# The output product of the mixers: attention's blocks first, other PSUM banks, weight splits on VectorE

## The chip, the cores and the metric

The kernel runs on one core of a Trainium2 chip. The core has a matrix engine (TensorE, PE in the rows, its weight loads PEld) and three engines for elementwise work: VectorE (DVE), ScalarE (ACT) and GpSimd (POOL). SyncE (SP) issues the DMA transfers. Each engine runs its own queue in order and waits for the others by semaphores. The metric is the device time of one execution in microseconds; lower is better.

## The reference, cut to what matters

Two decoder layers on 512 tokens of width 1024, in float32. A layer is four sub-steps, each between two RMS norms and added to x:

```python
x += 1/2 * post(swiglu_a(pre(x)))
h  = pre(x) @ W_in            # columns for attention | mLSTM | RWKV-7
x += post(concat(attn, mlstm, rwkv) @ W_out)
x += 1/2 * post(swiglu_b(pre(x)))
x += post(sigmoid(pre(x) @ W_g) * (p[l] @ W_p))
```

The concatenated output of the mixers has 1024 columns: 512 of attention, 256 of the mLSTM, 256 of RWKV-7. With the 1024 x 1024 matrix `W_out` it makes the output product, which is the place of the change.

## The kernel before, in words

Each float32 operand of a product is split in a high part, rounded to the reduced format fp32r, and a low rest. `split` (L138) has ScalarE round the high part (L139) and another engine, VectorE unless `eng` says GpSimd, subtract it (L140). `mm3` (L165) is then three matmuls: high by high (L167), high by low (L168), low by high (L169). Tokens lie in four tiles of 128.

The mixers of a layer run woven into each other (`weave`, L649): attention, RWKV's scan over chunks and the mLSTM each issue pieces in turn, each with PSUM banks of its own. There are eight banks, by tags: `m` has two, `r` three, and `o`, `a` and `b` one each. `lanes(main, aux)` sets the two cycles of tags from which `mm_tile` and `aux_tile` take the next bank; without arguments they are `mmoa` and `brrr` (L27). During the weave, attention uses `o`, `a` and `b`, the scan and the mLSTM `m` and `r`. The results are split into `yh` and `yl` (xh, xl in the rows), two chunks of 128 rows for each quarter of `W_out`: quarters 0 and 1 are attention's, 2 the mLSTM's, 3 RWKV's. RWKV's last steps are the norm (`rwkv_norm`, L952 to L957), transposes (`rwkv_back`, L964), a gate (L968 to L973) and the split into `yh` and `yl`; the mLSTM's last steps are L1206 to L1219 and its transposes, `pym` (L1136). Working data of all this lies in the `arena`, which is given back at the end.

`out_proj` (L262) makes the product in two halves of 512 output columns. For half 0 each of the four token tiles has an accumulator `y0`, for half 1 `y1`. In half 0 the first three blocks are loaded, split and multiplied with all four token tiles; the last block (`wot`) goes tile by tile, so that the tiles finish one after the other. In half 1 all four blocks go tile by tile; their raw weights `wor` lie in slots which overlap the arena, as do the raw weights `wr` of the next feed-forward, so both loads wait for the arena's last reader. `orders` in `mix` gives the order of the quarters in each half. `OW` (L31) has one letter for each block of half 0: with "1" the low half of its weights is made on GpSimd.

When a tile of y1 is done, `out_evac` squares and sums it on ScalarE (L196) and multiplies it by the gain on VectorE (L259); `postnorm` gets the factor r on GpSimd (`rms`, L185 and L186) and adds to x on VectorE (L254). Then `prenorm` squares and sums x (L196), gets r (L186), multiplies (L207, `xn`), and `turn` transposes (L218, `xtp`) and splits. For tiles 2 and 3, `turn` also makes sums of x (`xr`, `tx`: L239 to L242) and splits them for the feed-forward, whose products use sums of blocks in the manner of Strassen. There, for each unit of 128 columns, `gate` makes `p12`, `unit` makes the sums of weights (L355, L357, L358), splits them (`w75`, `w63`) and makes `p63`, `p75` and `p4`. `ffn_begin` loads the first units' weights (`wr`) and splits them (`w1`, the low halves on GpSimd).

The order of the instructions is not the program's: a scheduler orders them from its own timeline of the program, by when operands and buffers are ready in it. So an edit at one place can move instructions at others.

Of the kernel before, what the change touches and what calls it, by code (L numbers as in the profile page):

```python
# [27 lines left out]

CONSTS, NCONST = {}, 0
MX = 1  # L30
OW = "1111"  # L31
PL = "000021"
TORD = (0, 2, 1, 3)
FSEQ = [[(q[0], int(q[1:])) for q in f.split()] for f in ("P0 S3 S4 P1 S5 S6 P2 S7 S8 S9", "S6 S7 S8 S9 S3 S4 S5")]
# [38 lines left out]
class Trunk:  # L73
# [188 lines left out]
    def out_proj(self, nb, part, blocks, gain, scale, after, tail):  # L262

        half0 = []
        for h in range(2):
# [8 lines left out]
            for i in range(cut):  # L274
                w, a = self.wblock(blocks(h, i), "wo", eng=self.nc.gpsimd if h == 0 and OW[i] == "1" else None), part(h, i)
                for t in range(NT):
                    one(i, w, a, t)
            raws = [None] * nb
            if h and tail == nb:
                raws = [q[:, j] for q in [self.slot("q", [2, 1024], "wor") for _ in range(nb // 2)] for j in range(2)]  # L280
            rest = [(i, self.wblock(blocks(h, i), "wot", bool(h), raws[i], self.nc.gpsimd if (raws[i] is not None and OE[i] == "1" if h else OW[i] == "1") else None), part(h, i)) for i in range(cut, nb)]
            def finish(t):
                e = self.out_evac(ps[t], gain, h, scale)
                if h == 0:
                    half0.append(e)
                else:
                    self.postnorm(t, half0[t], e, scale)
                    self.late.append(after(t))
# [298 lines left out]
    def mix(self, l, after):  # L587
        nc, tc = self.nc, self.tc
        self.yh, self.yl = self.xh, self.xl
        self.close_slots()  # L590
        xd = self.dram.tile([NT, 128, D], F32, tag="xd", name="xd")
        for t in range(NT):
            nc.sync.dma_start(out=xd[t], in_=self.x[:, t])
        self.xs = self.x.rearrange("p a b -> p (a b)")
        with tc.tile_pool(name="arena", bufs=1) as pa:
            self.arena = pa.tile([128, 16384], F32, name="arena")
            cs = self.region(0, [SLOT])
            o = 0

            def load(n, ap):  # L600
                nonlocal o
                t = cs[:, o:o + n]
                nc.sync.dma_start(out=t, in_=ap)
                o += n
                return t

            self.pf = pf = load(38, self.ins["mix_cols"][l])
            self.consts = load(NCONST, self.ins["consts"])
            self.rows = load(272, self.ins["mix_rows"][l:l + 1].to_broadcast([128, 272]))
            self.gup = load(256, self.ins["rwkv_g_up"][l])  # L610
            self.om = om = cs[:, o:o + 10]
            assert o + 10 <= SLOT
            nc.vector.scalar_tensor_tensor(self.cen, self.const("bones"), -1.0 / 64, self.ident, ALU.mult, ALU.add)
            nc.vector.tensor_scalar(om[:, 0:8], pf[:, 0:8], -1.0, 1.0, op0=ALU.mult, op1=ALU.add)
            nc.vector.tensor_scalar(om[:, 8:10], pf[:, 14:16], -1.0, 1.0, op0=ALU.mult, op1=ALU.add)
            with tc.tile_pool(name="arena2", bufs=1) as pb:
                self.arena2 = pb.tile([128, 6144], F32, name="arena2")
                self.lanes("oab")
                self.attention_kv(l)
                with tc.tile_pool(name="keys", bufs=1) as pk:  # L620
                    self.bkt = pk.tile([128, 2048], F32, name="bk")
                    self.lanes("m", "r", "R")
                    self.rwkv_prep(l)
                    self.lanes("oab")
                    self.attention_q(l)
                    self.lanes("m", "r", "R")
                    self.mg = self.gains.tile([128, D], F32, tag="gain", name="mg")
                    self.rwkv_scores()
                with tc.tile_pool(name="parts", bufs=1) as pk:
                    self.parts = pk.tile([128, 2048], F32R, name="parts")  # L630
                    self.mlstm_proj(l)
                    self.weave(l)
        for t in range(NT):
            nc.sync.dma_start(out=self.x[:, t], in_=xd[t])
        self.open_slots()
        self.lanes()
        wo = self.ins["w_out"]
        post = self.gain("ln_mix_post", l)
        if not self.dbg:
            orders = ((2, 0, 1, 3), (3, 2, 0, 1))  # L640
            self.out_proj(4, lambda h, i: [[q[:, 2 * orders[h][i] + j] for q in (self.yh, self.yl)] for j in range(2)],
                          lambda h, i: wo[l, h, orders[h][i]], post, 1.0, after, 4)
        else:
            for t in range(8):
                o = self.ytile()
                nc.vector.tensor_tensor(o, self.yh[:, t].bitcast(F32), self.yl[:, t].bitcast(F32), ALU.add)
                nc.sync.dma_start(out=self.out[:, t], in_=o)
# [866 lines left out]
```

## Time and profile before

| | |
|---|---|
| median of 3 runs | 2187.12 us (2185.07 to 2189.22) |
| profiled execution | 2185.51 us |
| its span | 2183.8 us |
| granted clock of PE, mean | 0.989 |
| busy PE / DVE / ACT / POOL | 97% / 79% / 46% / 15% |

The times are the median of three runs; the trace is from one execution, whose own time is 1.6 us below the median. Its span goes from the first to the last instruction. A row of the timeline gives the start, the duration, engine, source line, operation and tiles; in square brackets stands how long the engine had been idle before it and what ended that. Rows that overlap on one engine are pipelined; the distance of their starts is what one costs.

### The profile page before, as it was taken

Reading aid. Unit: us, or ns where it says so; the run is one execution under the profiler, and the core shown is the slowest. Engines: PE = TensorE matmul, PEld = TensorE weight load, DVE = VectorE, ACT = ScalarE, POOL = GpSimd, SP = SyncE. Lnnn points to the kernel's source line nnn. Section 1 sums busy time; section 2 is a strip of 40 time slices with the busy share of each in tenths; the row PEclk is TensorE's granted clock in tenths of the full one; section 3 lists DMA queues with packets and bytes.
Section 4 is the critical chain, followed back from the end, with each engine's and each line's share of the span. In section 5 each row is a group of like instructions: output and inputs, shape, how many; then the busy total and the mean of one; then the engine's idle time right before and its main releaser. Section 6 shows DMA issues by size and latency. Waiting matters only on the chain.

```text
span 2183.8 us, 39815 instructions
## 1 busy us (share of the span) xinstructions
PE 2108.5 (97%) x16256; PEld 1959.2 (90%) x16256; DVE 1718.1 (79%) x2886; ACT 1007.5 (46%) x1653; POOL 330.5 (15%) x424
## 2 busy tenths in 40 slices
PE   6999999999988999999979999999999989999998
PEld 5999999888767999999879999998886789999996
DVE  8999977555768999977689999775557689999774
ACT  4444434446545444434554444345465454444343
POOL 4000011132235000011240000110422340000111
PEclk8999999999999999999989999999999999999999
DMA  4322214322031232224313222252210413222241
GB/s 164 117 97 99 86 68 154 122 71 57 21 141 53 103 111 97 88 68 165 115 58 117 97 98 78 79 178 97 64 54 12 155 59 117 97 97 78 78 143 71
DMA packets 67495, 208.62 MB, mean 96 GB/s; under 512 B 15728, under 2 KB 16752, under 8 KB 67312
## 3 DMA queue, kind: packets, MB, share of 16 engines
q1 hardware_dynamic: 67312, 206.07, 26.9%
q8 instruction: 128, 2.10, 0.4%
q14 instruction: 55, 0.45, 0.1%
HBM read 199.23 MB, written 6.82 MB: 94 GB/s over the span
## 4 chain that ended last, share of the span: by engine, by line
PE 81%; DVE 9%; ACT 3%; DMA 3%; issue 2%; POOL 2%; SPq 0%; DVEq 0%; POOLq 0%; ACTq 0%
PE y L463 18%; PE p L169 13%; PE p L168 13%; PE p L167 13%; PE pkrv L169 1%; PE pkrv L168 1%; PE pkrv L167 1%; PE y L167 1%; PE y L168 1%; PE y L169 1%; DVE xn L207 1%; DMA ws_r<-in_w_ffn_out 1%; DVE w L140 1%; PE pgt L168 1%; PE pgt L169 1%
## 5 line engine op out<-in xcount | busy, mean ns | idle before, releaser
L169 PE MATMUL p<-xh,w 128*128 128x256 f32 x1408 | 401.1, 286 | 7.5 <-POOL w L140 7.5
L167 PE MATMUL p<-xh,w 128*128 128x256 f32 x1408 | 401.2, 286 | 4.4 <-DVE gate L367 2.4
L168 PE MATMUL p<-xl,w 128*128 128x256 f32 x1408 | 401.1, 285 | 0.4 <-DVE xl L140 0.4
L167 PE MATMUL p<-tx,w 128*128 128x256 f32 x1056 | 295.9, 284 | 9.6 <-ACT tx L139 8.0
L168 PE MATMUL p<-tx,w 128*128 128x256 f32 x1056 | 295.3, 283 | 6.5 <-DVE tx L140 6.5
L169 PE MATMUL p<-tx,w 128*128 128x256 f32 x1056 | 294.9, 283 | 2.5 <-DVE w L140 2.5
L169 PEld LDWEIGHTS p<-xh,w 128*128 128x128 f32 x1408 | 271.9, 193 | 8.1 <-POOL w L140 8.1
L167 PEld LDWEIGHTS p<-xh,w 128*128 128x128 f32 x1408 | 271.7, 194 | 6.7 <-DVE gate L367 3.2
L168 PEld LDWEIGHTS p<-xl,w 128*128 128x128 f32 x1408 | 271.9, 193 | 1.4 <-DVE xl L140 1.3
L139 ACT ACTIVATE w<-ws 128x1024 fp32r<-128x1024 f32 x176 | 185.9, 1056 | 159.0 <-PE p L169 144.2
L140 DVE TENSOR_TENSOR w<-ws,w 128x1024 fp32r<-128x1024 f32 x176 | 221.3, 1257 | 15.8 <-ACT w L139 15.0
L167 PEld LDWEIGHTS p<-tx,w 128*128 128x128 f32 x1056 | 201.7, 192 | 12.0 <-ACT tx L139 9.2
L168 PEld LDWEIGHTS p<-tx,w 128*128 128x128 f32 x1056 | 201.9, 192 | 7.5 <-DVE tx L140 7.5
L169 PEld LDWEIGHTS p<-tx,w 128*128 128x128 f32 x1056 | 200.6, 191 | 2.8 <-DVE w L140 2.8
L139 ACT ACTIVATE w<-wr 128x512 fp32r<-128x512 f32 (+1 forms) x176 | 147.8, 844 | 113.8 <-PE p L169 66.7
L463 PE MATMUL y<-wo,hq 128*128 128x256 f32 x1536 | 193.3, 283 | 0.0
L463 PEld LDWEIGHTS y<-wo,hq 128*128 128x128 f32 x1536 | 186.4, 190 | 0.8
L499 POOL TENSOR_TENSOR tb<-tb,ln_ffn_post 128x512 f32<-128x512 f32 x16 | 24.1, 1530 | 1076.5 <-ACT junk L196 1076.5
L463 PE MATMUL y<-ws_r,h 128*128 128x256 f32 x672 | 158.4, 379 | 0.2
L140 DVE TENSOR_TENSOR w<-wr,w 128x512 fp32r<-128x512 f32 (+1 forms) x161 | 151.4, 943 | 5.6 <-ACT w L139 4.7
L463 PEld LDWEIGHTS y<-ws_r,h 128*128 128x128 f32 x672 | 121.2, 189 | 14.7 <-DMA ws_r<-in_w_ffn_out 0.8
L351 ACT ACTIVATE gate<-p 128x256 f32<-128x256 f32 x88 | 33.1, 381 | 171.6 <-PE p L169 169.4
(426 smaller groups left out, 4766.8 us busy)
## 6 DMA issues: line engine op xcount, KB each, us to landing
wr<-in_w_ffn_in SPq DMA_DIRECT2D x176, 512.0 KB, 4.1
ws_r<-in_w_ffn_out SPq DMA_DIRECT2D x56, 512.0 KB, 3.3
wo_r<-in_w_ffn_out SPq DMA_DIRECT2D x32, 512.0 KB, 3.3
pkrv_r<-in_w_rw SPq DMA_DIRECT2D x16, 512.0 KB, 3.5
wpg_r<-in_w_ple_gate SPq DMA_DIRECT2D x16, 512.0 KB, 4.0
xd<-x SPq DMA_DIRECT2D x8, 512.0 KB, 2.8
x<-xd SPq DMA_DIRECT2D x8, 512.0 KB, 3.5
pq_r<-in_w_q SPq DMA_DIRECT2D x8, 512.0 KB, 3.5
```

Of the source, the lines that this page charges most:

```text
L139: self.nc.scalar.activation(hi, src, AF.Copy)
L140: (eng or self.nc.vector).tensor_tensor(lo, src, hi.bitcast(F32), ALU.subtract)
L167: mm(out, a[0], b[0], start=first, stop=False)
L168: mm(out, a[0], b[1], start=False, stop=False)
L169: mm(out, a[1], b[0], start=False, stop=last)
L207: v_.scalar_tensor_tensor(xn[:, h], self.x[:, t, h], r, gain[:, h], ALU.mult, ALU.mult)
L351: a_.activation(a[:, (H, L)[m % 2]], pa[:, L], AF.Copy)
L463: nc.tensor.matmul(banks[n][:, u], x, y, start=n not in seen, stop=last and i == len(todo) - 1, skip_group_check=True)
L499: (g_ if not h or QL[0] == "1" else v_).tensor_tensor(tb, tb, gain[:, h * 512:h * 512 + 512], ALU.mult)
```

## The change

Three edits, in both layers. The letters of `OW` become "0000": the low halves of half 0's four weight blocks are made on VectorE. The order of half 0's quarters becomes 0, 1, 3, 2 (attention, attention, RWKV, mLSTM) from 2, 0, 1, 3. And the accumulators get other banks: y0 of tiles 0 to 3 in `o`, `a`, `b`, `m` (before `m`, `m`, `o`, `a`), y1 in `m`, `r`, `r`, `r` (before `b`, `r`, `r`, `r`); after the product the lanes are set back.

```diff
-OW = "1111"
+OW = "0000"
...
-        self.lanes()
+
+        self.lanes("oabm", "mrrr")
         wo = self.ins["w_out"]
         post = self.gain("ln_mix_post", l)
         if not self.dbg:
-            orders = ((2, 0, 1, 3), (3, 2, 0, 1))
+            orders = ((0, 1, 3, 2), (3, 2, 0, 1))
             self.out_proj(4, lambda h, i: [[q[:, 2 * orders[h][i] + j] for q in (self.yh, self.yl)] for j in range(2)],
                           lambda h, i: wo[l, h, orders[h][i]], post, 1.0, after, 4)
+            self.lanes()
```

The lines of the kernel after are one higher from L637 and two higher from L644 on. In the rows below the number behind a name tells its uses apart: `y0_6809` to `y0_6812` are half 0's sums of token tiles 0 to 3 in layer 0, `wo_6815`, `wo_6844` and `wo_6873` its first three blocks of weights.

On PE, at the end of the mixers of layer 0. Before, the product begins behind the last step of the RWKV scan (`py_6693`) and the mLSTM's transposes:

```order
L925 MATMUL py_6693<-st_6033,arena_4195 64x128
L905 MATMUL pq_6688<-st_6033,arena_4195 64x128
L1172 MATMUL pnum_6763<-vg_5176,arena_4195 128x128 x3
L1178 MATMUL pint_6768<-arena_4195 128x130 x2
L927 MATMUL py_6693<-arena2_4206 64x64 x2
L925 MATMUL py_6693<-st_6033,arena_4195 64x128
L927 MATMUL py_6693<-arena2_4206 64x64 x2
L1136 MATMUL pym_6787<-ident_78,mg_4923 128x128 x2
L167 MATMUL y0_6811<-wo_6815,xh_87 128x512
L168 MATMUL y0_6811<-wo_6815,xh_87 128x512
```

After, it begins further up, at attention's last values (`po_5990`), ahead of the state steps `pq_6627` and `py_6641` of the scan, of which two more follow:

```order
L917 MATMUL pst_6626<-st_6033,ident_78 64x128
L1370 MATMUL po_5990<-arena_4195 64x512
L167 MATMUL y0_6810<-wo_6815,xh_87 128x512
L168 MATMUL y0_6810<-wo_6815,xh_87 128x512
L169 MATMUL y0_6810<-wo_6815,xl_88 128x512
L167 MATMUL y0_6810<-wo_6815,xh_87 128x512
L168 MATMUL y0_6810<-wo_6815,xh_87 128x512
L169 MATMUL y0_6810<-wo_6815,xl_88 128x512
L167 MATMUL y0_6810<-wo_6844,xh_87 128x512
L168 MATMUL y0_6810<-wo_6844,xh_87 128x512
L169 MATMUL y0_6810<-wo_6844,xl_88 128x512
```

Thirty-six products of attention's two blocks with tiles 0 to 2 now stand ahead of the scan's last step, at four places, and 12 of the third block behind it, ahead of RWKV's transposes `pyt`. Behind the mLSTM's last transposes 174 products of both halves stood, now 144.

On DVE, between the product and the second feed-forward (`tb` is L259's product of y1 with the gain, `x_86` the sum of L254, `xn` the norm of the next sub-step for tiles 1 and 2, `xl_88` the split of transposed x). Before:

```order
L259 TENSOR_TENSOR tb_7158<-y1_6951,ln_mix_post_6807 128x512
L207 SCALAR_TENSOR_TENSOR xn_7114<-x_86,r_7111,ln_ffn2_pre_7030 128x512 x2
L140 TENSOR_TENSOR xl_88<-xtp_7117,xh_87 128x4x128
L254 SCALAR_TENSOR_TENSOR x_86<-tb_6939,r_7164,x_86 128x512
L254 SCALAR_TENSOR_TENSOR x_86<-tb_7158,r_7164,x_86 128x512
L140 TENSOR_TENSOR xl_88<-xtp_7122,xh_87 128x4x128
L259 TENSOR_TENSOR tb_7228<-y1_6952,ln_mix_post_6807 128x512
L207 SCALAR_TENSOR_TENSOR xn_7179<-x_86,r_7176,ln_ffn2_pre_7030 128x512 x2
L140 TENSOR_TENSOR xl_88<-xtp_7182,xh_87 128x4x128
L254 SCALAR_TENSOR_TENSOR x_86<-tb_6944,r_7234,x_86 128x512
```

After:

```order
L207 SCALAR_TENSOR_TENSOR xn_7114<-x_86,r_7111,ln_ffn2_pre_7030 128x512 x2
L140 TENSOR_TENSOR xl_88<-xtp_7122,xh_87 128x4x128
L259 TENSOR_TENSOR tb_7158<-y1_6951,ln_mix_post_6807 128x512
L254 SCALAR_TENSOR_TENSOR x_86<-tb_6939,r_7164,x_86 128x512
L254 SCALAR_TENSOR_TENSOR x_86<-tb_7158,r_7164,x_86 128x512
L140 TENSOR_TENSOR xl_88<-xtp_7182,xh_87 128x4x128
L207 SCALAR_TENSOR_TENSOR xn_7179<-x_86,r_7176,ln_ffn2_pre_7030 128x512 x2
L140 TENSOR_TENSOR xl_88<-xtp_7187,xh_87 128x4x128
L259 TENSOR_TENSOR tb_7228<-y1_6952,ln_mix_post_6807 128x512
L254 SCALAR_TENSOR_TENSOR x_86<-tb_6944,r_7234,x_86 128x512
L254 SCALAR_TENSOR_TENSOR x_86<-tb_7228,r_7234,x_86 128x512
```

The product L259 of tiles 2 and 3 stood ahead of the norm of the tile before it and now stands behind it.

On DVE, at the start of the second feed-forward (`tx_7208` is the split of the sums for token tiles 2 and 3, `ws_7477` and `ws_7478` are unit 1's sums of weights, `w75_7394` and `w63_7397` unit 0's splits, `w75_7482` unit 1's). Before:

```order
L140 TENSOR_TENSOR tx_7208<-tx_7211,tx_7208 128x4x128
L140 TENSOR_TENSOR xl_88<-xtp_7203,xh_87 128x4x128
L140 TENSOR_TENSOR w75_7394<-ws_7389,w75_7394 128x1024
L239 TENSOR_TENSOR xr_7127<-xr_7127,xtp_7287 128x512
L355 TENSOR_TENSOR ws_7477<-wr_7081 128x1024
L240 SCALAR_TENSOR_TENSOR tx_7297<-xtp_7292,xr_7127 128x512
L241 TENSOR_TENSOR tx_7298<-xtp_7292,tx_7298 128x512
L140 TENSOR_TENSOR w63_7397<-ws_7390,w63_7397 128x1024
L140 TENSOR_TENSOR tx_7208<-tx_7297,tx_7208 128x4x128
L140 TENSOR_TENSOR xl_88<-xtp_7292,xh_87 128x4x128
L357 TENSOR_TENSOR ws_7478<-ws_7477,wr_7081 128x512
L140 TENSOR_TENSOR w75_7482<-ws_7477,w75_7482 128x1024
```

After:

```order
L140 TENSOR_TENSOR tx_7208<-tx_7211,tx_7208 128x4x128
L140 TENSOR_TENSOR xl_88<-xtp_7203,xh_87 128x4x128
L140 TENSOR_TENSOR w75_7394<-ws_7389,w75_7394 128x1024
L355 TENSOR_TENSOR ws_7477<-wr_7081 128x1024
L140 TENSOR_TENSOR w63_7397<-ws_7390,w63_7397 128x1024
L239 TENSOR_TENSOR xr_7127<-xr_7127,xtp_7287 128x512
L357 TENSOR_TENSOR ws_7478<-ws_7477,wr_7081 128x512
L240 SCALAR_TENSOR_TENSOR tx_7297<-xtp_7292,xr_7127 128x512
L241 TENSOR_TENSOR tx_7298<-xtp_7292,tx_7298 128x512
L140 TENSOR_TENSOR w75_7482<-ws_7477,w75_7482 128x1024
L358 TENSOR_TENSOR ws_7478<-ws_7478,wr_7081 128x512
L140 TENSOR_TENSOR tx_7208<-tx_7297,tx_7208 128x4x128
```

The sums L357 and L358 and the split `w75_7482` of unit 1 stood behind the last split of `tx_7208` and now stand ahead of it; all of unit 0's splits now stand ahead of L239. On SP the loads of the gains `ln_mix_post` and `ln_ffn2_pre` stood behind the first and the fourth load of `wor`, and now stand ahead of all four. On POOL the four splits of half 0's weights are gone.

## Rows read from the trace of the kernel before

All stretches are of layer 0, but for groups 7 and 8 and the page's row.

**Rows 1.** The page's table of busy time: of each engine the us, the share of the span and the number of instructions.
```profile
PE 2108.5 (97%) x16256; PEld 1959.2 (90%) x16256; DVE 1718.1 (79%) x2886; ACT 1007.5 (46%) x1653; POOL 330.5 (15%) x424
```

**Rows 2.** Windows of the span: start and end, length, then busy us and number of instructions of PE, PEld, DVE, ACT and POOL, the granted clock, the DMA engines' busy share and GB/s.
```profile
600.00:627.00 27.00, 24.65 (x262) 18.59 (x256) 19.55 (x65) 12.98 (x42) 7.50 (x8) 1.00 0.04 9
627.00:650.00 23.00, 18.76 (x82) 14.71 (x83) 13.23 (x21) 8.64 (x13) 8.56 (x5) 1.00 0.63 232
...
680.00:720.00 40.00, 34.96 (x258) 33.45 (x259) 39.80 (x48) 22.13 (x36) 17.71 (x12) 0.91 0.23 79
```

**Rows 3.** Timeline of PE from the end of the mixers into half 1 of the output product.
```profile
627.66 0.50 PE L167 MATMUL y<-wo,xh 128*128 128x512 f32 x1 [0.89 <-ACT xh L139]
...
633.28 0.66 PE L964 MATMUL pyt<-ident,x 128*128 128x128 f32 x4 [1.94 <-DVE x L957]
...
637.48 0.44 PE L1136 MATMUL pym<-ident,mg 128*128 128x128 f32 x2 [1.52 <-POOL mg L1219]
...
650.03 0.40 PE L167 MATMUL y<-wot,xh 128*128 128x512 f32 x1
...
672.05 1.04 PE L218 MATMUL xtp<-ident,xn 128*128 128x128 f32 x8
```

**Rows 4.** Timeline of DVE, ACT and POOL at the end of the RWKV scan and behind it, with an earlier row of L957.
```profile
606.42 0.69 DVE L957 TENSOR_TENSOR x<-x,rs 128x512 f32<-128x512 f32 x1
...
626.40 0.28 ACT L928 ACTIVATE x<-py 128x128 f32<-128x128 f32 x1 [2.88 <-PE py L927]
...
630.32 2.36 POOL L140 TENSOR_TENSOR wo<-wo_r,wo 128x1024 fp32r<-128x1024 f32 x1
630.38 2.85 DVE L957 TENSOR_TENSOR x<-x,rs 128x512 f32<-128x512 f32 x1 [0.42 <-POOL rs L177]
...
636.43 0.42 DVE L140 TENSOR_TENSOR xl<-arena,xh 128x256 fp32r<-128x256 f32 x1
```

**Rows 5.** Timeline of SP, ACT, POOL, DVE and PE from the loads of `wor` to the norms ahead of the second feed-forward.
```profile
636.94 0.33 SPq L156 DMA_DIRECT2D wor<-in_w_out  x1
...
649.55 1.06 ACT L139 ACTIVATE w<-wr 128x1024 fp32r<-128x1024 f32 x1 [0.92 <-DMA wr<-in_w_ffn_in]
650.74 6.25 POOL L140 TENSOR_TENSOR w<-wr,w 128x1024 fp32r<-128x1024 f32 x2 [0.48 <-ACT w L139]
...
659.80 2.42 POOL L140 TENSOR_TENSOR w<-wr,w 128x1024 fp32r<-128x1024 f32 x1 [2.81 <-ACT w L139]
...
663.33 1.41 DVE L254 SCALAR_TENSOR_TENSOR x<-tb,r,x 128x512 f32<-128x512 f32 x2 [0.60 <-POOL r L186]
...
666.88 1.41 DVE L207 SCALAR_TENSOR_TENSOR xn<-x,r,ln_ffn_pre 128x512 f32<-128x512 f32 x2 [2.14 <-POOL r L186]
...
673.05 0.69 DVE L259 TENSOR_TENSOR tb<-y,ln_mix_post 128x512 f32<-128x512 f32 x1 [2.50 <-ACT junk L196]
...
678.43 1.03 PE L218 MATMUL xtp<-ident,xn 128*128 128x128 f32 x8
679.41 0.69 DVE L259 TENSOR_TENSOR tb<-y,ln_mix_post 128x512 f32<-128x512 f32 x1 [1.82 <-ACT junk L196]
...
683.86 0.68 DVE L239 TENSOR_TENSOR xr<-xr,xtp 128x512 f32<-128x512 f32 x1
```

**Rows 6.** Timeline of DVE and PE at the start of the second feed-forward.
```profile
699.70 1.75 DVE L140 TENSOR_TENSOR tx<-tx 128x512 fp32r<-128x512 f32 x1
...
701.51 0.58 PE L168 MATMUL p<-tx,w 128*128 128x256 f32 x1 [1.27 <-DVE tx L140]
...
701.98 1.17 DVE L357 TENSOR_TENSOR ws<-ws,wr 128x512 f32<-128x512 f32 x1
703.07 2.30 DVE L140 TENSOR_TENSOR w<-ws,w 128x1024 fp32r<-128x1024 f32 x1
...
704.45 0.29 PE L167 MATMUL p<-tx,w 128*128 128x256 f32 x1
...
705.89 0.41 DVE L367 TENSOR_TENSOR gate<-p,gate 128x256 f32<-128x256 f32 x1
```

**Rows 7.** Timeline of DVE and PE at the start of the first feed-forward of layer 1.
```profile
1103.54 0.69 DVE L239 TENSOR_TENSOR xr<-xr,xtp 128x512 f32<-128x512 f32 x1 [1.02 <-ACT tx L238]
...
1118.77 0.68 DVE L357 TENSOR_TENSOR ws<-ws,wr 128x512 f32<-128x512 f32 x1
1119.37 1.22 DVE L140 TENSOR_TENSOR w<-ws,w 128x1024 fp32r<-128x1024 f32 x1
1120.50 0.68 DVE L240 SCALAR_TENSOR_TENSOR tx<-xtp,xr 128x512 f32<-128x512 f32 x1
...
1121.70 0.68 DVE L358 TENSOR_TENSOR ws<-ws,wr 128x512 f32<-128x512 f32 x1
1122.30 2.29 DVE L355 TENSOR_TENSOR ws<-wr 128x1024 f32<-128x1024 f32 x1
1124.51 1.75 DVE L140 TENSOR_TENSOR tx<-tx 128x512 fp32r<-128x512 f32 x1
...
1126.32 0.58 PE L168 MATMUL p<-tx,w 128*128 128x256 f32 x1 [2.75 <-DVE tx L140]
...
1131.16 0.28 PE L167 MATMUL p<-xh,w 128*128 128x256 f32 x1
```

**Rows 8.** Timeline of PE at the start of the second feed-forward of layer 1.
```profile
1783.53 0.58 PE L168 MATMUL p<-tx,w 128*128 128x256 f32 x1 [1.27 <-DVE tx L140]
```

## The prediction

> **What bounds the kernel now.** I read the page first, then a table of windows, then the timelines around the output product. The page is to show that TensorE (PE) sets the time: it is busy in 97% of the span, VectorE (DVE) in 79% [rows 1]. So an edit counts only where PE waits. The windows show where that is, in layer 0, around the edit: the end of the mixers (600 to 627 us) leaves PE 27.00 − 24.65 = 2.35 us free, the start of the output product (627 to 650) 23.00 − 18.76 = 4.24 us, the start of the second feed-forward (680 to 720) 40.00 − 34.96 = 5.04 us, there with a granted clock of 0.91 and DVE busy for 39.80 of 40 us [rows 2]. The PE timeline names three of the waits in the product's start: 0.89 us for the split of the mLSTM's values, 1.94 for the RWKV norm's multiplication on DVE (L957) and 1.52 for GpSimd's (POOL's) multiplication at L1219 [rows 3]. The restart of the feed-forward stands at 701.51 us, behind the DVE split of the last sum of x (`tx`, L140) [rows 6]. The same restart in layer 1 is at 1783.53 [rows 8], so layer 1 repeats layer 0 1082.02 us later, and I work out one layer and take it twice.
>
> **1. Attention's products move into the scan.** By the order of PE, 36 products of blocks 0 and 1 with token tiles 0 to 2 now stand ahead of the last RWKV chunks. Ninety-six products lie between 650.03 and 672.05, so one takes 22.02 / 96 = 0.229 us [rows 3]; 36 take 8.2 us. Their cover would be PE's idle time in the scan. It closes between none and all of those 2.35 us [rows 2]; I take 0.7, nearer to none, because the order puts them at four places only. So the scan's last chunk ends 8.2 − 0.7 = 7.5 us later (5.9 at the least): 626.40 [rows 4] becomes about 634 us. PE itself loses nothing by that; these products are no longer to be done later. But RWKV's tail hangs on it.
>
> **2. The tail after the scan.** Before, from the last chunk's evacuation on ScalarE (626.40) to the last split that reads the arena on DVE (end 636.43 + 0.42 = 636.85) it is 10.45 us [rows 4]. In it L957 took 2.85 us, beside POOL's split of `wo` (630.32, 2.36 us); without POOL beside it the same row took 0.69 at 606.42 [rows 4]. The splits leave POOL, so I take off 2.16. `wo_6873`'s split now stands in that stretch on DVE itself; the nearest rows of DVE splits of this size are 1.22 alone [rows 7] and 2.30 beside POOL [rows 6], mostly in a gap in which DVE waits for POOL's `rs`, so I add 0.6 (0 to 2.3). Sum 8.9 us: the arena is free at about 634.0 + 8.9 = 642.9, 6 us later than before.
> For PE: its wait of 0.89 goes. In its place it waits for the third block's low half and for L957, together about 1.9, and 0.7 for L1219 in place of 1.52. The last transpose of the mLSTM then starts at about 640.7 (637.48 before) with 144 products behind it (174 before). 640.7 + 144 × 0.229 + 1.6 (transposes and small waits) = 675.3, where the last y1 product ended before 678.43 [rows 5]. The product ends 3.1 us earlier per layer: this is the gain of the change.
>
> The Trainium skill, page "SBUF — State Buffer", section "Who interferes with whom", says that a VectorE instruction with two SBUF operands and a GpSimd instruction that reads SBUF share one read interface, and that the second to issue waits until the first is done. The trace agrees: 2.85 against 0.69 us for L957. By that rule the change would be good wherever a DVE row stood beside POOL's splits, which the 2.16 above already holds; it also says that the three rows of step 4 will be dear if POOL works beside them.
>
> **3. From the product to the feed-forward.** That gain has to pass through the chain of norms. The loads of `wor` and `wr` go to slots that overlap the arena; the first was issued at 636.94, right after the last reader, and the first ScalarE split of `wr` waited for its transfer until 649.55 [rows 5]. Now they start 6 us later, but the two gains are loaded ahead of them. The window's 232 GB/s [rows 2] over its 23 us is 5.3 MB, ten transfers of 512 KB (the size of each of these loads) in the 13 us from 636.94 to 650, 1.3 us each; two are 2.6. So the first `wr` split is some 3.4 us later. POOL's three splits of w1 (6.25 us for two, one of 2.42) stand ahead of the first norm on POOL in both kernels; the third ended at 659.80 + 2.42 = 662.22, after a wait of 2.81 for ScalarE [rows 5]. That wait is spent: 649.55 + 1.2 + 3.4 + 6.25 + 2.42 = 662.8. POOL's norm, and with it DVE's L254 of tile 0, comes at about 663.8 (663.33 before). From there DVE had waited 2.50 and 1.82 us for sums of squares of y1 [rows 5], which an earlier y1 closes. But by the new order the product of tile t + 1 (L259) and its L254 stand behind the norm xn of tile t, and each xn waits for squares on ScalarE and r on POOL after its L254: 2.14 us in the one row that shows it, at 666.88 [rows 5]. Three pitches of 1.33 (L254) + 2.14 + 1.33 (L207) + 0.6 (L259), 5.4 and with splits of xl 5.9, end in L239 at about 663.8 + 3 × 5.9 + 2 = 683.4; before 683.86. So of 3.1 us 0.5 arrive. Bounds: all 3.1, if POOL's w1 splits start no later; 2 us of loss, if they start the whole 6 us later.
>
> **4. The restart.** In DVE's order three rows of unit 1 now stand ahead of the last split of tx: the two sums L357 and L358 and the split of w75. PE in order needs that split, and nothing is left to run before it: the products for p12 are out. The three cost 701.98 to 705.89, 3.91 us, where they stood beside POOL [rows 6]; at the start of the first feed-forward of layer 1, where DVE has this order already, their pitches are 0.60, 1.13 and 0.60, 2.33 us [rows 7]. After the change POOL is still in its splits of tx beside them for part: 3.0 us.
> PE then restarts colder. Before, 13 products ran at half clock from 701.51 to 704.45 (0.21 against 0.12 us of pitch) [rows 6]; after the longer idle time of layer 1's analog 22 did, 1126.32 to 1131.16 [rows 7]. Nine more are 9 × 0.093 = 0.85; I take 0.4, the middle.
>
> **5. The weave.** POOL's first two splits leave the scan, DVE's come in, two rows of 1.2 us or so among about 40 us of DVE work per 60 us. L957's example bounds the gain by 2 × 2.16, the loss by 2 × 2.30 [rows 4, 6]; PE has work there, so 0, ±1.
>
> Sum per layer: −0.5 + 3.0 + 0.4 = +2.9, twice +5.8 us. The profiled execution took 2185.51 us (span 2183.8 and 1.7 around it): 2191.3. It lies 1.6 us below the median 2187.12 of the runs shown, so I predict 2193 us.
>
> **Rivals.**
> (B) The gain arrives. If ScalarE's squares and POOL's r run ahead (y1 is out 3 us earlier, so the ScalarE queue is freer) and the three rows of step 4 lie in time in which DVE waits anyway, each layer gains 3 to 4 us: 2187.1 − 7 = 2180. For it: 4.24 us of waits in the product's start, which no other work owns. Against it: DVE is busy 39.80 of 40 us [rows 2], so no gap is seen in which rows could lie. It decides where DVE's L239 of tile 3 comes over 3 us earlier.
> (C) Parts cancel: steps 3 and 4 come out at −2 and +2.3, within noise: about 2187.
> (D) Slower still: the restart becomes like that of layer 1's first feed-forward, where from L239 of tile 2 (1103.54) to the end of the last tx (1126.26) it took 22.7 us [rows 7] against 17.6 here (683.86 [rows 5] to 701.45 [rows 6]): +5.1 per layer and half-clock products, or y1 also waits for the late `wor`: +6 per layer, 2199.
> (E) The change doesn't do what it says: the order shows that it does, so no chance of its own.
>
> **How the numbers follow.** A 0.47, B 0.2, C 0.21, D 0.12. A difference under 0.2% (4.4 us) can't be told from none. A lies at +6 and spreads over 2189 to 2196: about two thirds of it slower, a third same. Faster: B 0.2. Same: C 0.21 + 0.17 of A = 0.38. Slower: 0.30 + 0.12 = 0.42. Range: from within B, 2181, to D's 2199; for A alone 2188 to 2196.
>
> **What would show it.** Step 1: the last evacuation at L928 near 634 instead of 626.4. Step 2: L957 near 0.7 us; last y1 product near 675. Step 3: L254 of tile 0 near 663.8, L239 of tile 2 near 683.4. Step 4: L357, L140 and L358 between L239 of tile 3 and the last tx, PE restarting some 3 us later than 701.5, for longer at half clock. The forecast is wrong if PE restarts before 701; that would be B.

## The result, and the profile after

The changed kernel takes 2209.47 us (median of 4 runs, 2208.52 to 2209.64), the kernel before 2187.49 in the same comparison: ratio 1.0103, 95% interval 1.0091 to 1.0115, or 22 us more. The forecast was 2193 with a range up to 2199: the sign was right, the size not. The profiled execution took 2209.64 us, span 2207.6.

The page after: busy times as in [rows 1], then the shares of the chain that ended last.

```profile
PE 2118.5 (96%) x16256; PEld 1962.6 (89%) x16256; DVE 1724.8 (78%) x2894; ACT 1004.9 (46%) x1653; POOL 315.8 (14%) x416
...
PE 75%; DVE 12%; DMA 4%; ACT 4%; issue 3%; POOL 2%; SPq 0%; DVEq 0%; POOLq 0%; ACTq 0%
```

TensorE (PE) has the same 16256 instructions as before, and the largest shift of busy time is GpSimd's (POOL's), 14.7 us less without the splits of half 0. PE's share of the last chain is 75%, on the page of before it was 81%, and VectorE (DVE), the DMA and ScalarE have more. No work was added. Of the 23.8 us by which the span is longer, PE stands idle in 13.8 and is busy longer with the same instructions in 10.0; its mean granted clock is 0.984 in place of 0.989.

Windows of the kernel after, with the columns of [rows 2]:

```profile
600.00:627.00 27.00, 25.71 (x235) 18.94 (x234) 16.50 (x50) 11.71 (x36) 7.12 (x8) 1.00 0.00 1
627.00:650.00 23.00, 20.55 (x123) 16.19 (x122) 13.04 (x35) 6.25 (x14) 4.52 (x4) 0.93 0.34 118
...
680.00:720.00 40.00, 28.08 (x194) 26.70 (x193) 33.72 (x37) 21.68 (x40) 18.96 (x15) 0.83 0.15 53
```

The end of the mixers (600 to 627 us) is fuller than before, as intended by products that start early: 25.71 us busy in place of 24.65. What is paid stands in the third row: from 680 to 720 PE is busy 28.08 us in place of 34.96, at a granted clock of 0.83 in place of 0.91, and now DVE has idle time there too (33.72 in place of 39.80).

Timeline of the engines from the first early product to the last product of half 1, the places of [rows 3 and 4]:

```profile
615.33 0.50 PE L167 MATMUL y<-wo,xh 128*128 128x512 f32 x1
...
635.67 0.28 ACT L930 ACTIVATE x<-py 128x128 f32<-128x128 f32 x1 [0.39 <-PE py L929]
...
637.61 0.86 PE L167 MATMUL y<-wo,xh 128*128 128x512 f32 x2 [1.97 <-ACT wo L139]
...
637.83 2.54 POOL L177 TENSOR_TENSOR rs<-var,mhalf 128x8 f32<-128x8 f32 x1 [10.55 <-DVE var L957]
...
638.92 0.79 PE L168 MATMUL y<-wo,xh 128*128 128x512 f32 x1 [0.46 <-DVE wo L140]
...
640.39 0.69 DVE L959 TENSOR_TENSOR x<-x,rs 128x512 f32<-128x512 f32 x1 [0.99 <-POOL rs L177]
...
642.50 0.60 PE L966 MATMUL pyt<-ident,x 128*128 128x128 f32 x4
...
643.80 0.38 PE L1138 MATMUL pym<-ident,mg 128*128 128x128 f32 x2
...
645.78 1.80 SPq L156 DMA_DIRECT2D wor<-in_w_out  x4
...
678.56 0.40 PE L169 MATMUL y<-wot,xl 128*128 128x512 f32 x1
```

The first product is issued at 615.33, 12.3 us earlier than before. The scan's last evacuation comes at 635.67 in place of 626.40, the first load of `wor` behind the arena's last reader at 645.78 in place of 636.94. The norm's multiplication (L959, L957 before) takes 0.69 us in place of 2.85, as forecast. The third block's split on ScalarE makes PE wait 1.97 us and, a little further on, its split on DVE another 0.46; the product behind that (638.92) takes 0.79 us in place of 0.40, and the granted clock of the window from 627 to 650 us is 0.93 in place of 1.00. GpSimd's `rs`, the factor for the norm, takes 2.54 us in place of 1.74. RWKV's transposes `pyt` start at 642.50, 1.42 us after L959 is done, behind the third block's products. The last product of half 1 starts at 678.56: no earlier than before. The two rows of before:

```profile
628.61 1.74 POOL L177 TENSOR_TENSOR rs<-var,mhalf 128x8 f32<-128x8 f32 x1 [3.54 <-DVE var L955]
...
678.20 0.40 PE L169 MATMUL y<-wot,xl 128*128 128x512 f32 x1
```

From the first split of `wr` to the sums of tile 2, the places of [rows 5]:

```profile
656.54 1.06 ACT L139 ACTIVATE w<-wr 128x1024 fp32r<-128x1024 f32 x1
...
657.73 8.63 POOL L140 TENSOR_TENSOR w<-wr,w 128x1024 fp32r<-128x1024 f32 x3 [15.06 <-DMA wr<-in_w_ffn_in]
...
666.46 0.63 POOL L185 TENSOR_SCALAR v<-ss_post,ss_post 128x1 f32<-128x1 f32 x1
...
667.78 1.42 DVE L254 SCALAR_TENSOR_TENSOR x<-tb,r,x 128x512 f32<-128x512 f32 x2 [0.26 <-POOL r L186]
...
671.10 1.42 DVE L207 SCALAR_TENSOR_TENSOR xn<-x,r,ln_ffn_pre 128x512 f32<-128x512 f32 x2 [1.91 <-POOL r L186]
...
686.76 0.69 DVE L239 TENSOR_TENSOR xr<-xr,xtp 128x512 f32<-128x512 f32 x1 [0.54 <-ACT tx L238]
```

GpSimd's three splits of w1 now start at 657.73 and end at 666.36; the norm of tile 0 waits for them, and L254 comes 4.45 us later than before. From L254 to L239 it takes 18.98 us in place of 20.53.

The restart of the second feed-forward, the places of [rows 6]:

```profile
690.72 4.62 DVE L207 SCALAR_TENSOR_TENSOR xn<-x,r,ln_ffn_pre 128x512 f32<-128x512 f32 x2
...
691.93 2.86 POOL L140 TENSOR_TENSOR w<-wr,w 128x1024 fp32r<-128x1024 f32 x1
...
701.57 0.68 DVE L239 TENSOR_TENSOR xr<-xr,xtp 128x512 f32<-128x512 f32 x1
...
702.16 0.69 DVE L357 TENSOR_TENSOR ws<-ws,wr 128x512 f32<-128x512 f32 x1
...
703.96 1.38 DVE L140 TENSOR_TENSOR w<-ws,w 128x1024 fp32r<-128x1024 f32 x1
...
705.27 1.75 DVE L358 TENSOR_TENSOR ws<-ws,wr 128x512 f32<-128x512 f32 x1
...
706.94 1.75 DVE L140 TENSOR_TENSOR tx<-tx 128x512 fp32r<-128x512 f32 x1
...
708.75 0.58 PE L168 MATMUL p<-tx,w 128*128 128x256 f32 x1 [2.92 <-DVE tx L140]
...
712.97 0.37 PE L167 MATMUL p<-tx,w 128*128 128x256 f32 x1
```

The norm of tile 3 (L207) takes 4.62 us for its two instructions. L357, the split of w75 and L358 stand between L239 of tile 3 and the last split of tx, and PE restarts at 708.75 in place of 701.51. Its products are at half clock until 712.97 (the granted clock is 0.50 from 708.70 to 713.00, the lower of its two levels, 1.2 GHz).

The output of the second feed-forward, where before no wait over 0.4 us was:

```profile
924.64 0.41 DVE L372 TENSOR_TENSOR gate<-p,gate 128x256 f32<-128x256 f32 x1
...
925.11 1.63 PE L463 MATMUL y<-wo,hq 128*128 128x256 f32 x12 [1.71 <-DVE gate L372]
```

PE waits 1.71 us for DVE's L372, which reads the last unit's accumulator p63. The page's group of these products has 5.7 us of waits for L372, in the three feed-forwards behind the change.

Later restarts and the end of the scan in layer 1:

```profile
1135.43 0.58 PE L168 MATMUL p<-tx,w 128*128 128x256 f32 x1 [2.75 <-DVE tx L140]
...
1728.85 0.28 ACT L930 ACTIVATE x<-py 128x128 f32<-128x128 f32 x1 [0.39 <-PE py L929]
...
1804.56 0.58 PE L168 MATMUL p<-tx,w 128*128 128x256 f32 x1 [2.92 <-DVE tx L140]
```

With the rows of before, this is where the time goes:

| event | before | after | later by |
|---|---|---|---|
| scan's last evacuation, layer 0 | 626.40 | 635.67 | 9.27 |
| first load of `wor` | 636.94 | 645.78 | 8.84 |
| L254 of tile 0 | 663.33 | 667.78 | 4.45 |
| L239 of tile 2 | 683.86 | 686.76 | 2.90 |
| restart, second feed-forward | 701.51 | 708.75 | 7.24 |
| restart, first feed-forward of layer 1 | 1126.32 | 1135.43 | 9.11 |
| scan's last evacuation, layer 1 | 1708.41 | 1728.85 | 20.44 |
| restart, second feed-forward of layer 1 | 1783.53 | 1804.56 | 21.03 |
| end of the span | 2183.8 | 2207.6 | 23.8 |

Three things are to be explained: the scan's delay, of which part comes back; a second loss at the restart; and some 2 us per feed-forward that arise far from the edit.

### The profile page after: what moved, and what is told of

The parts are those of the page before. It is cut to its first block, busy times and chain, and to the rows that moved or that the text cites. A ratio compares the mean times of both kernels' runs of the same rounds, so it can differ in the third digit from the quotient of the medians.

```text
span 2207.6 us, 39818 instructions
## 1 busy us (share of the span) xinstructions
PE 2118.5 (96%) x16256; PEld 1962.6 (89%) x16256; DVE 1724.8 (78%) x2894; ACT 1004.9 (46%) x1653; POOL 315.8 (14%) x416
## 4 chain that ended last, share of the span: by engine, by line
PE 75%; DVE 12%; DMA 4%; ACT 4%; issue 3%; POOL 2%; SPq 0%; DVEq 0%; POOLq 0%; ACTq 0%
PE y L463 15%; PE p L167 12%; PE p L168 12%; PE p L169 12%; DMA ws_r<-in_w_ffn_out 2%; DVE xn L207 1%; PE pkrv L169 1%; PE pkrv L168 1%; PE pkrv L167 1%; DVE w L140 1%; PE pgt L168 1%; ACT junk L196 1%; PE pgt L169 1%; PE pgt L167 1%; PE po L1370 1%
```

## The experiments

In the comparisons that follow the kernel before took between 2186.87 and 2188.94 us, so ratios are compared rather than times.

**The edits one by one.** e1 has only the letters of `OW`, e2 only the order of the quarters, e3 only the lanes with their setting back, e4 the first two:

```diff
e1: -OW = "1111"                              +OW = "0000"
e2: -orders = ((2, 0, 1, 3), (3, 2, 0, 1))    +orders = ((0, 1, 3, 2), (3, 2, 0, 1))
e3: -self.lanes()                             +self.lanes("oabm", "mrrr")
    (behind out_proj)                         +self.lanes()
e4: e1 and e2
```

> Only the first edit: the low halves of half 0's weights on VectorE, block order and banks as before. The order has no product of the output product ahead of the scan's end and the restart of the second feed-forward as before. Theory (the loss comes from products put ahead of the scan and from the three rows of unit 1 ahead of the last tx split, not from the engine of the weight splits): within 4 us of before, 2183 to 2191. Rival (the splits on VectorE cost the time): over 2200.

> Only the block order 0, 1, 3, 2. The order has 24 products ahead of the scan's end instead of 36, and the restart of the feed-forward as before. Theory: 24 x 0.229 = 5.5 us of delay to the scan per layer, of which 1 to 3 arrive at the restart, no cost of unit 1's rows: 2189 to 2195. Rival (early products cost the whole of their time at the end of the mixers): over 2197. Rival (the restart's order makes the whole loss): 2187.

> Only the banks: y0 in o, a, b, m. The order has 24 products ahead of the scan's end and 54 ahead of RWKV's transposes, and unit 1's rows stand ahead of the last tx split, as in the changed kernel. Theory: most of the loss comes with this edit, 2200 to 2210, PE restarting 6 us or more later than before in layer 0. Rival (the block order or the splits make it): under 2193.

> First and second edit without the banks. The order has 24 products ahead of the scan's end, in layer 0 the restart as before, in layer 1 unit 1's rows ahead of the last tx split. Theory: layer 0 as with the block order alone, layer 1 some 3 to 5 us worse than layer 0: 2190 to 2199. Rival (the splits on VectorE cost the time): over 2203.

| | median us | ratio to before | 95% interval |
|---|---|---|---|
| e1, splits on VectorE | 2179.95 | 0.9966 | 0.9954 to 0.9979 |
| e2, block order | 2194.71 | 1.0037 | 1.0024 to 1.0050 |
| e3, banks | 2202.64 | 1.0072 | 1.0057 to 1.0087 |
| e4, splits and block order | 2203.39 | 1.0073 | 1.0058 to 1.0088 |

The splits on VectorE are not the loss: alone they make the kernel 7 us faster, more than the theory expected (its range was missed). e1's timeline in layer 0, with the scan's last evacuation, L957 and the restart:

```profile
628.42 0.28 ACT L928 ACTIVATE x<-py 128x128 f32<-128x128 f32 x1 [2.87 <-PE py L927]
...
632.40 0.69 DVE L957 TENSOR_TENSOR x<-x,rs 128x512 f32<-128x512 f32 x1
...
700.82 0.58 PE L168 MATMUL p<-tx,w 128*128 128x256 f32 x1 [2.41 <-DVE tx L140]
```

L957 takes 0.69 us here too. (e1's profiled execution took 2186.35 us, the longest of its six, so the whole gain can't be read from it.) The block order alone (e2) costs 8 us, at the upper end of what the theory had. Its scan ends, and its second feed-forward restarts, at

```profile
632.22 0.28 ACT L928 ACTIVATE x<-py 128x128 f32<-128x128 f32 x1 [0.39 <-PE py L927]
...
706.95 0.39 PE L168 MATMUL p<-tx,w 128*128 128x256 f32 x1 [1.27 <-DVE tx L140]
```

The scan ends 5.82 us later than before, where 24 early products are 5.5 us. The restart is 5.44 us later, so nearly all of the delay arrives there; the theory had 1 to 3. The banks alone (e3), 24 early products and the new restart, have these two rows at

```profile
632.69 0.28 ACT L929 ACTIVATE x<-py 128x128 f32<-128x128 f32 x1 [0.39 <-PE py L928]
...
706.24 0.58 PE L168 MATMUL p<-tx,w 128*128 128x256 f32 x1 [3.27 <-DVE tx L140]
```

The scan ends 6.29 us later and the restart comes 4.73 later, where 6 or more were expected; the time is in the theory's range. e4 was expected under 2199 and came out at 2203, just in the range of its rival, by which the splits on VectorE cost the time; alone (e1) they gain, but with the block order they come with 8 us more than the order alone. In e4, by the shift of its rows against before, layer 0 ends 3 us later and layer 1 another 12, where the order has 51 products ahead of RWKV's transposes, against 24 in layer 0. The edits don't add: each changes the order that the scheduler makes of the whole.

**The far loss: which banks the feed-forward gets.** Reading the code for a reason for the wait on L372: `out_proj` takes four banks of the cycle `brrr` for y1 and six for the transposes of tiles 0 to 2, which its `flush` calls make. Ten is two beyond two whole cycles. Setting the lanes back behind it starts the cycle anew, so all accumulators after it fall two places further: the last unit's p63 gets `b`, which the first sum of the feed-forward's output also takes (`y0_1`, written to bank `b` by name). e5 keeps the change and steps the cycle on by two, e6 is the kernel before with the setting back alone:

```diff
e5 (changed kernel):              self.lanes()
                                 +next(self.aux), next(self.aux)
e6 (kernel before), behind out_proj:
                                 +self.lanes()
```

> The changed kernel, but after the lanes are set back the auxiliary cycle is stepped on by two, so that the banks of the feed-forward's accumulators fall as before the change. Theory (setting the lanes back shifted the cycle brrr by two; by that the last unit's p63 gets bank b, which y0_1 of the feed-forward's output needs, and PE waits there 2.0 to 2.5 us in three feed-forwards): 2209.5 - 6.9 = 2202 to 2204, and no wait of the first y of the feed-forward's output for L372. Rival (these waits come from the delay ahead of them): 2207 to 2211.

> The kernel before with only the second setting back of the lanes, behind the output product: the same shift of the cycle, nothing else. Theory: 2.0 to 2.5 us in each of three feed-forwards, 2187 + 6.9 = 2193 to 2195. Rival: 2187.

e6: 2196.58 us, ratio 1.0032 (1.0019 to 1.0045), 7 us more, with an interval of 4 to 10. PE's waits in its three later feed-forward outputs (total us, times, longest):

```profile
PE y L463 <- DVE gate L372: 1.9, 1, 1.9
PE y L463 <- DVE gate L372: 2.3, 1, 2.3
PE y L463 <- DVE gate L372: 1.7, 1, 1.7
```

The kernel before has none of them. e5: 2208.49 us, ratio 1.0085 (1.0068 to 1.0102). The three waits are gone from its trace, but the gain of 4 us is short of the 6.9 expected and inside the intervals: in layer 1 its order put 60 products ahead of RWKV's transposes in place of 48, and its rows are late by more, in layer 0 too (restart at 711.54 in place of 708.75). In layer 0 other waits, up to 0.77 us long, stand in place of the one that is gone. So the mechanism is shown by e6, whose rows agree with those of before within 0.3 us up to the second feed-forward, and by the waits that go in e5; e5's time doesn't show the gain.

**The restart.** e7 is e5 with unit 1's sums held behind the last split of tx:

```diff
             sx, sy = (self.wraw.tile([128, 1024], F32, tag="raw", name="ws") for _ in range(2))
+            if m == 1 and w == 2:
+                v_.tensor_copy(sx[:, 0:4], self.tx[0][:, 1, 3, 252:256].bitcast(F32))
```

> The changed kernel with the cycle stepped on by two, and in the second feed-forwards the sums of unit 1 held behind the last split of tx by a copy of 4 columns from that split into the sum's buffer (it is overwritten). Theory (three rows of unit 1 ahead of the last tx split cost 3 to 4 us at each restart): 6 to 8 us below the kernel with the cycle alone stepped on, 2194 to 2197. Rival (the norms' chain sets the restart, or the rows come due later anyway): within 2 us of it, 2201 to 2204.

e7: 2199.62 us, ratio 1.0046 (1.0029 to 1.0063): 8.5 us below e5 by the ratios, a little more than the theory's 6 to 8. Its timeline at the restart:

```profile
690.74 0.69 DVE L239 TENSOR_TENSOR xr<-xr,xtp 128x512 f32<-128x512 f32 x1 [0.55 <-ACT tx L238]
...
704.31 0.67 DVE L239 TENSOR_TENSOR xr<-xr,xtp 128x512 f32<-128x512 f32 x1
...
706.51 1.04 DVE L140 TENSOR_TENSOR tx<-tx 128x512 fp32r<-128x512 f32 x1
...
707.61 0.58 PE L168 MATMUL p<-tx,w 128*128 128x256 f32 x1 [0.69 <-DVE tx L140]
```

From L239 of tile 2 to the restart it takes 707.61 − 690.74 = 16.9 us, in the changed kernel 708.75 − 686.76 = 22.0 (22.0 in e5 too), before 17.6. The rival (the norms set the restart) has fallen: the rows of unit 1 delay the restart. The hold moves four of them, the three and the sum L355 ahead of them, which stood ahead of the last split of tx before the change as well; so e7 gives the price of the four, 5.1 us, not that of the three.

**The early products.** e9 is the changed kernel with half 0's weight splits held behind the mLSTM's last but one split, so that no product of y0 can stand ahead of the scan's end. e10 is e7 with the same hold: block order, banks and splits of the change stay, and the three suspects are out.

```diff
 w = self.wsp.tile([128, 2, src.shape[1]], F32R, tag="w", name=name)
+if name == "wo" and self.hold is not None:
+    self.nc.vector.tensor_copy(w[:, 0, 0:4], self.hold)
...
 half0 = []
+self.hold = self.yl[:, 4, 380:384].bitcast(F32)
```

> The changed kernel with the splits of half 0's first three weight blocks held behind the mLSTM's last but one split (a copy of 4 columns of it into the weights' buffer, overwritten by the split). By the order no product of y0 stands ahead of the scan's end any more, and one row less ahead of the last tx split. Theory (each product ahead of the scan's last steps delays the end of the mixers by its whole time, 36 x 0.229 = 8.2 us per layer, since the chain from the scan's end to the restart sets the time and PE's later work is not on it): the scan's last evacuation 8 us earlier than in the changed kernel, the time 2190 to 2197. Rival (PE's work is the same, so what is done early is not done late; the loss sits behind the product): 2205 to 2211.

> The same with the cycle stepped on by two and unit 1's sums held behind the last tx split: all three suspected costs are out of the changed kernel, its block order, banks and splits stay. Theory: 2178 to 2186, no slower than before. Rival (something else of the change costs too): over 2190.

e9: 2199.07 us, ratio 1.0056 (1.0041 to 1.0071), 10 us below the changed kernel, 2 us above the range expected. Its scan, sums of tile 2 (now L241) and restart:

```profile
625.22 0.28 ACT L934 ACTIVATE x<-py 128x128 f32<-128x128 f32 x1 [2.87 <-PE py L933]
...
682.64 0.67 DVE L241 TENSOR_TENSOR xr<-xr,xtp 128x512 f32<-128x512 f32 x1
...
703.83 0.58 PE L170 MATMUL p<-tx,w 128*128 128x256 f32 x1 [2.38 <-DVE tx L140]
```

The scan ends 10.5 us earlier than in the changed kernel (625.22 against 635.67), the sums of tile 2 come 4.1 us earlier; the restart still takes 21.2 us from them, with the rows of unit 1 in front, and the far loss is still in. Part of the 10.5 is not the products': the hold also takes the splits of the first two blocks out of the weave, and rows of the scan at 580 to 605 us lie 2.1 us earlier than in the changed kernel. e10: 2182.01 us, ratio 0.9978 (0.9969 to 0.9987):

```profile
624.65 0.28 ACT L937 ACTIVATE x<-py 128x128 f32<-128x128 f32 x1 [2.87 <-PE py L936]
...
637.41 1.75 SPq L158 DMA_DIRECT2D wor<-in_w_out  x4
...
682.04 0.68 DVE L241 TENSOR_TENSOR xr<-xr,xtp 128x512 f32<-128x512 f32 x1
...
698.63 0.58 PE L170 MATMUL p<-tx,w 128*128 128x256 f32 x1 [1.26 <-DVE tx L140]
```

In layer 0 the scan, the norms and the restart lie 1.8 to 2.9 us earlier than before, the first load half a microsecond later; the restart takes 16.6 us from the sums of tile 2. Against e7 the hold alone is worth 0.0068 of the time, 15 us in two layers; 36 products of 0.229 us are 8.2 per layer, 16.5. The two can't be set equal, as the hold also moves splits out of the weave, whose rows lie 2.5 us earlier for that in layer 0. With these three out, nothing of the loss is left, and the change is 5 us faster than before. That is no more than the splits on VectorE gain alone (e1, 7 us): no run shows a gain from the block order or the banks.

**What lies between.** e11 gives w1's low halves to VectorE in the changed kernel, e12 gives half 0's back to GpSimd:

```diff
e11: -EW1 = self.nc.gpsimd      +EW1 = None if w == 2 else self.nc.gpsimd
e12: -OW = "0000"               +OW = "1111"
```

> The changed kernel with the low halves of the second feed-forward's first weights (w1) on VectorE instead of GpSimd. Theory (GpSimd's splits of w1 hold the factor r of the first norm): L254 of tile 0 comes 2 to 4 us earlier than 667.78, the restart 1 to 3, the time 2203 to 2208. Rival (VectorE is full there, four splits of 1.2 us lengthen its queue by as much): 2209 to 2217.

> The changed kernel with half 0's low halves on GpSimd again (block order and banks changed). The order has the same 36 products ahead of the scan's end and the same three rows at the restart. Theory (the splits on VectorE cost 0.9 us in the weave and gain about 4 at the end of the mixers, per layer): 3 us per layer above the changed kernel, 2212 to 2219. Rival (the splits on VectorE cost time): below 2207.

e11: 2204.71 us, ratio 1.0083 (1.0064 to 1.0101), in the range of the theory, though its interval overlaps that of the changed kernel. In layer 0:

```profile
666.52 1.41 DVE L254 SCALAR_TENSOR_TENSOR x<-tb,r,x 128x512 f32<-128x512 f32 x2
...
706.38 0.58 PE L168 MATMUL p<-tx,w 128*128 128x256 f32 x1 [3.35 <-DVE tx L140]
```

L254 is 1.26 us earlier, not 2 to 4, and the restart 2.4 us: GpSimd's splits hold the norms, but not alone. e12: 2211.42 us, ratio 1.0110 (1.0095 to 1.0125), 1.5 us above the changed kernel and within its interval, where 6 us were expected. What the splits on VectorE gain alone (e1) they hardly gain behind 36 early products.

**A faster version.** e8 is e1 with the hold of e7, in the first feed-forward of layer 1 too:

```diff
+            if m == 1 and l + w > 1:
+                v_.tensor_copy(sx[:, 0:4], self.tx[0][:, 1, 3, 252:256].bitcast(F32))
```

> The kernel before with the low halves on VectorE (the first edit alone, 2180) and unit 1's sums held behind the last split of tx in the second feed-forwards and in the first one of layer 1. In that one, three rows stand ahead of the last split, in the others one. Theory: 1 us less in each second feed-forward and 3 to 4 in the first of layer 1: 2174 to 2177. Rival (DVE has no slack behind the restart, the rows are only late there): 2179 to 2182.

e8: 2179.56 us, ratio 0.9961 (0.9946 to 0.9976), as fast as e1 and faster than both kernels. That the hold gains nothing beside e1 is the rival's result; why its earlier restart in layer 1 doesn't show in the time stays open.

## Why the prediction was wrong

The sum per layer was −0.5 + 3.0 + 0.4 = +2.9. The profile shows +7.24 at the restart of layer 0, and about 12 us per layer at the end. What failed is step 3's term, with the gain of step 2 in it: L239 of tile 2 was to come 0.5 us earlier and came 2.9 later, because the weights' loads were 7.0 us late at their first split, not 3.4, and the 3.1 us of gain at the end of the product did not exist. The banks of the feed-forward, some 3 us per layer, were in no term at all. Point by point:

- **Step 1, early products.** 8.2 us less 0.7 of cover. Measured, the scan's end moved 9.27 us; 0.9 of it was there at 580 to 605 us already (the weave, step 5), so 8.4: no cover at all. e2 and e3 agree with 24 products (5.82 and 6.29 for 5.5), e9 takes it all back. The mechanism was right, its cover was mis-sized by 0.7.
- **Step 2, the tail.** Forecast 8.9 us from the last evacuation to the arena's last reader. From 635.67 to the first load of `wor` at 645.78 it is 10.1; before it was 10.5. L957's gain of 2.16 came to the tenth (0.69 us), and nearly all of it was given back at two places. GpSimd's `rs` took 2.54 us, beside DVE's split of the third block, in place of 1.74. And L959's result, done at 641.08, lay until 642.50, as PE had the 12 products of the third block to do first; before, the transposes followed L957 at once. PE stood at its last mLSTM transposes at 643.80, not 640.7, and needed 34.8 us from there as forecast (34.6). The 640.7 doesn't follow from the terms beside it: before, those transposes came 11.08 us behind the scan; with the waits put in as forecast and six products fewer ahead of them it is 8.0, which from 634.0 gives 642.0, and from the scan's measured end 643.6. **So the 3.1 us of gain at half 1's end, the only gain of the forecast, did not exist**: 678.56 against 678.20 before.
- **Step 3, from the product to the feed-forward.** This is the step that failed most. L254 was put at 663.8 and came at 667.78. The delay of the loads was forecast as 6 − 2.6 = 3.4 us at the first split of `wr`; it was 656.54 − 649.55 = 7.0: 8.84 at the first load, handed on by steps 1 and 2, of which 1.85 in place of 2.6 was won back by that split. POOL's splits followed at once, 657.73. The step took the wait of 2.81 us in POOL's splits as slack, and rightly: with 7.0 for 3.4 its own sum gives 666.4 for their end, and 666.36 was measured. So the term that was mis-sized is the delay of the loads, and a delay of 7 us used the slack up. The chain of norms behind it was right (forecast 19.6 us from L254 to L239, measured 18.98), so L239 was +2.9 in place of −0.5.
- **Step 4, the restart.** Forecast 3.0 + 0.4. Measured 22.0 − 17.6 = 4.3 us between L239 and the restart, and 20 half-clock products in place of 13 (708.75 to 712.97 at 0.21 us), 0.7 more. The three rows stand where the forecast put them, and by the distances of their starts they cost 0.60, 1.31 and 1.67 us, 3.6 in place of 3.0. The part that the forecast didn't have is L207 of tile 3: 4.62 us in place of 3.5, as it now meets POOL's split of w (691.93, 2.86 us), which before came behind it. The Trainium skill, page "SBUF — State Buffer", section "Who interferes with whom", says that two SBUF operands on VectorE contend with GpSimd's reads; the trace agrees, as the same two instructions took 1.42 us at 671.10.
- **Step 5, the weave.** 0 ± 1; measured 0.9. Every kernel whose splits go to VectorE within the weave (e1, e4, e5, e7, e8, e11) loses 0.7 to 0.9 us of layer 0 there, with early products or without; e2, e3 and e12, with the splits on GpSimd, nothing over 0.1.
- **Missing: the banks of the feed-forward.** No step and no rival had it. The diff showed the added `self.lanes()`, and the text of the change said that the lanes are set back; I took that as no edit, without counting the uses of the cycle. It cost 5.7 us of waits in the changed kernel's trace and 7 us in e6, between a quarter and a third of the whole.

Of the rivals, D had the restart's mechanism and size (+5.1 per layer) but not the scan's full delay or the banks. With the steps at their measured sizes, layer 0 is: scan 9.27, given back up to L239 6.37, restart 4.3, half clock 0.7, banks 1.7: 9.6, where the next feed-forward starts 9.11 us late. Layer 1 adds the banks of its first feed-forward (2.2) and gives back less between scan and norms.

## What to carry to other kernels

A queue that is 97% busy can still be the waiting one where it matters: look for the serial chain (here scan, last reader of a buffer, loads, splits, norms, restart) and ask of every product put ahead of it whether its time is saved on that chain or only later, off it. Here early independent work found no idle time to fill: put in whole blocks ahead of a chain, it delayed the chain by all of its time. Whether smaller pieces would have fitted was not tried. And count the uses of every round-robin (banks, buffers) that an edit resets: a shift by two places here cost a quarter to a third of the loss, first seen some 200 us behind the edit.

## What the runs showed of the hardware that was not expected

Four splits of 1.2 us per layer moved from GpSimd to VectorE, the busier engine (79% against 15%), made the kernel before 7 us faster (e1). What is seen for it is that beside one of GpSimd's splits a single row of VectorE took 2.85 in place of 0.69 us; beside others, in the changed kernel, a pair took 4.62 in place of 1.42. That this alone makes the 7 us was not tried apart. Nor is it a rule: with the new block order the same move came with 8 us more (e4 against e2), and with all edits it made no difference clear of the intervals (e12).
